# Own pools for the first two weight tiles behind each norm, converted ahead of the norm on VectorE

## The chip, the core and the metric

The kernel runs on one core of a Trainium2 chip. Five engines work there side by side, each on an instruction stream of its own: TensorE (PE) multiplies matrices, VectorE (DVE), ScalarE (ACT) and GpSimd (POOL) work element by element, and SyncE (SP) issues most of the transfers. Engines wait for each other by semaphores, and each takes its own instructions strictly in order. The metric is the device time of one execution in microseconds (us); lower is better.

## The reference

One inference step of a small recurrent decoder: 528 prompt positions (16 meta tokens and 512 new ones) and 8 running sequences of 8 tokens, so 592 positions with 1024 channels. Layer 0 has an S5 mixer, layer 1 a gated linear recurrence (RG-LRU). A post-norm and a gated feed-forward net with a causal width-3 convolution follow each mixer:

```python
mix = s5_mixer(h, ...)  or  rglru_mixer(h, ...)
h = layer_norm(DN_ALPHA * h + mix, g0, b0)
up = h @ w_up                                    # 1024 -> 2 * 2816
upc, new_hist = causal_dwconv(up, hist, conv_w, conv_b)
f = (gelu(upc[..., 2816:]) * upc[..., :2816]) @ w_down
h = layer_norm(DN_ALPHA * h + f, g1, b1)
```

All is float32, and the outputs are the hidden states and the new recurrent and convolution states.

## The kernel before

The kernel keeps activations transposed: a tile holds 128 channels by 592 positions, eight tiles (`RES`) hold the residual. Columns are worked in two halves of about 296. To get float32 accuracy from TensorE, each operand is cut into two parts, `hi` and `lo`; a product of two tiles is three matmuls (lines 151 to 153): `hi*hi`, `lo*hi` and `hi*lo`. Weights come as raw float32 tiles of 128 x 8 x 128 (`wraw`, a ring of three, loaded on SP's queue). Their `whi` is a copy on ScalarE (`convert_hi`, line 122), their `wlo` a subtraction (`convert_lo`, line 131), on VectorE unless the caller names GpSimd; both have rings of four. `keys` lists the weight tiles in the order of use; `load(to)`, `convert(to)` and `pump` work down that list to a given place, and `weights(key)` hands out the next.

There are four norms: behind the S5 mixer (I call it norm 0), behind the first feed-forward net (norm 1), behind the RG-LRU (norm 2), and the last. The first three are followed by another product. `skewed` (line 1005) writes the order by hand (`tc.manual_schedule`) so that one half of the columns is normed while TensorE works on the other half. Its steps:

- the first halves of the last `tail` tiles of the product (four, in norm 0 two) and their evacuation into `RES` (`evac`). `norm.add` squares each on ScalarE (L902) and adds up values and squares on GpSimd (L906, L907);
- the second halves on TensorE, and between them the totals over channels (`mean`, `square`: L920, L922);
- `centered` (line 924): mean and variance on ScalarE (L930, L931, L936) and VectorE (L934, L935, L951 to L955), the mean taken off `RES` (L940 on GpSimd, L945 on VectorE). `late` is called behind L936;
- `applied` (line 982): for each of eight tiles the scaling on VectorE (L973), `hi` on ScalarE (L974) and `lo` on VectorE (L979). `plan` says what stands behind tile k: the evacuations of the second halves, and conversions of weights;
- the first three output tiles of the next product (`nxt`, kept in `opened`): the first two take each `hi`, `lo` pair as it comes, with the totals of the second half behind the fifth pair, then the third; then `centered` and `applied` for the second half, and the second half of the three outputs.

Before the change, the weights of these three outputs are converted inside the norm: `whi` of the first two in `late`, and their `wlo` by `plan`, two on GpSimd in norm 0, one on GpSimd and one on VectorE in norms 1 and 2. The third is converted behind tile 5 or 6, its `wlo` on GpSimd. That makes seven conversions on GpSimd, 181 on VectorE.

Each feed-forward net opens a pool of its own (`ffn`, line 1125). Its first tile, `hist`, is loaded on ScalarE's queue (L1134) and prepared by four operations on GpSimd (L1138 to L1141); L1161 adds it to the convolution's result, and the gelu (L1166) follows. Behind each of the first three norms, GpSimd adds an offset to the eight tiles of `RES` (L1002). Outside `skewed` a scheduler sets each engine's order.

Of the kernel before, what the change touches and what calls it, by code (L numbers as in the profile page):

```python
# [9 lines left out]
F32R = mybir.dt.float32r  # L10
I32 = mybir.dt.int32
AF = mybir.ActivationFunctionType
ALU = mybir.AluOpType

P = 128
# [50 lines left out]
def trunk(tc, x, xn, s5p, s5bc, smp, fhist, w5i, w5o, wri, wrg, wro, wup, wdn, o_y, o_s5, o_rgh, o_rgc, o_ffc):  # L66
    nc = tc.nc
    V, G, A, T = nc.vector, nc.gpsimd, nc.scalar, nc.tensor
    with ExitStack() as ctx:
# [33 lines left out]
        keys = [("s5in", m) for m in range(DM)]  # L103
        for m in range(DM):
            keys += [("s5out", m), ("s5out", m + DM)]
        keys += ffn_keys(0) + rg_keys() + ffn_keys(1)
        raw, ready = {}, {}
        at = {"load": 0, "hi": 0, "conv": 0, "get": 0}

        def load(to):  # L110
            while at["load"] < min(to, len(keys)):
# [3 lines left out]
                raw[at["load"]] = (t, kk)  # L115
                at["load"] += 1

        def convert_hi(to):
            while at["hi"] < min(to, len(keys)):
                t, kk = raw[at["hi"]]  # L120
                hi = wp.tile([P, 8, P], F32R, tag="whi", name="whi", bufs=4)
                A.activation(hi[:, 0:kk, :], t[:, 0:kk, :], AF.Copy)  # L122
                ready[at["hi"]] = [hi, None]
                at["hi"] += 1

        def convert_lo(to, eng=V):
            while at["conv"] < min(to, len(keys)):
                t, kk = raw.pop(at["conv"])
                hi = ready[at["conv"]][0]
                lo = wp.tile([P, 8, P], F32R, tag="wlo", name="wlo", bufs=4)  # L130
                eng.tensor_tensor(lo[:, 0:kk, :], t[:, 0:kk, :], hi[:, 0:kk, :].bitcast(F32), op=ALU.subtract)  # L131
                ready[at["conv"]][1] = lo
                at["conv"] += 1
# [871 lines left out]
        def skewed(ms, prod, evac, norm, cols, hl, nxt, n, cuts, plan, slots=None, out=None, tail=4):  # L1005

            body, end = ms[:-tail], ms[-tail:]
            for m in body:
                if slots is not None:
                    whole(slots, m, cols)
                for f in (lambda h: prod(m, h, 0, n), lambda h: evac(m, h)):
                    for h in (0, 1):
                        f(h)

            def pair(i, h):
                if slots is not None and i < 2:  # L1020
                    ps = psum()
                    for j in (0, 1):
                        slots[end[i + 2 * j], h] = ps[:, 512 * j:512 * j + cols[h][1] - cols[h][0]]

            opened = []
            turn = list(order)
            with tc.manual_schedule():
                for i, m in enumerate(end):
                    pair(i, 0)
                    prod(m, 0, 0, n, ahead=i < tail // 2)  # L1030
                    evac(m, 0)
                load(at["conv"] + 3)
                A.activation(scr, scr, AF.Abs_reciprocal_sqrt)
                m = end[0]
                pair(0, 1)
                prod(m, 1, 0, cuts[0])
                norm.pst = psum()
                norm.mean(cols[0])
                prod(m, 1, cuts[0], cuts[1])
                norm.square(cols[0])  # L1040
                prod(m, 1, cuts[1], n)
                pair(1, 1)
                prod(end[1], 1, 0, n)
                early = (lambda: evac(m, 1)) if tail == 4 else None
                norm.centered(cols[0], late=plan.get("late"), early=early)
                if tail == 4:
                    prod(end[2], 1, 0, n)

                def second(i):
                    evac(end[i], 1)  # L1050
                    if tail == 4 and i == 1:
                        prod(end[3], 1, 0, n)

                todo = {k: [f if callable(f) else lambda i=f: second(i) for f in fs]
                        for k, fs in plan.items() if isinstance(k, int)}
                norm.applied(cols[0], hl, out, todo)
                c = cols[0]
                for i, key in zip((turn[1], turn[3]), nxt):
                    opened.append((psum(i), weights(key, False)))
                norm.pst = psum(turn[2])  # L1060
                for k in range(DM):
                    for o in opened:
                        part(*o, hl, c, k, k + 1, k == 0, k == DM - 1)
                    if k == 4:
                        norm.mean(cols[1])
                        norm.square(cols[1])
                if nxt:
                    opened.append((psum(turn[0]), weights(nxt[2], False)))
                    part(*opened[2], hl, c)
                order.remove(turn[2])  # L1070
                order.insert(0, turn[2])
                norm.centered(cols[1], lambda: A.activation(scr, scr, AF.Abs_reciprocal_sqrt))
                norm.applied(cols[1], hl, out)
                if nxt:
                    load(at["conv"] + 3)
                    convert(at["conv"] + 1)
                c = cols[1]
                for k in range(4):
                    for o in opened:
                        part(*o, hl, c, k, k + 1, k == 0, False)  # L1080
                for o in opened:
                    part(*o, hl, c, 4, DM, False, True)
            if hl is not None:
                norm.offsets(cols[0][0])
            return opened
# [10 lines left out]
        def convert(to, eng=V):  # L1096
            convert_hi(to)
            convert_lo(to, eng)
# [9 lines left out]
        def glu_evac(m, h):  # L1108
# [8 lines left out]
        HL1 = hltiles()  # L1117
        up_first = lambda l: [("up", l, m) for m in (0, FT, 1)]
        opened = skewed(list(range(DM)), glu_prod, glu_evac, norm, FULL, HL1, up_first(0), DM, (4, 4),
                        {"late": lambda: (A.activation(scr, scr, AF.Tanh), convert_hi(at["conv"] + 2)),  # L1120
                         0: [lambda: convert_lo(at["hi"], G)], 1: [0], 3: [1],
                         5: [lambda: convert(at["conv"] + 1, G)]}, tail=2)


        def ffn(l, *args):
# [3 lines left out]
        def ffn_in(fp, l, HL, u0, d0, i_norm, hl_out, opened, nxt, out):  # L1129
# [57 lines left out]
            for g, (k0, k1) in enumerate(GROUPS):  # L1187
# [44 lines left out]
                                PLAN if nxt else {0: [1], 3: [2], 4: [3]}, slots, out)  # L1232
            return hl, opened

        PLAN = {"late": lambda: convert_hi(at["conv"] + 2),
                0: [lambda: convert_lo(at["conv"] + 1, G), 1, lambda: convert_lo(at["conv"] + 1)],
                3: [2], 4: [3], 6: [lambda: convert(at["conv"] + 1, G)]}
        HL2, opened = ffn(0, HL1, 0, 0, 1, True, opened, [("rgin", DM + m) for m in range(3)], None)


# [151 lines left out]
        for m in range(3):  # L1392
            for h in (0, 1):
                ro_prod(m, h, DM - 2, DM)
            for h in (0, 1):
                ro_evac(m, h)
        HL3 = hltiles()
        opened = skewed(list(range(3, DM)), ro_prod, ro_evac, norm, gcols, HL3, up_first(1), DM, (4, 6), PLAN, slots)
        nc.sync.dma_start(o_rgc, rgc)
        nc.sync.dma_start(o_rgh, rgh)  # L1400
        rgs.close()

        pairs = {}

# [100 lines left out]
```

## Time and profile before

| what | before |
|---|---|
| median of 3 runs | 1402.8 us (1402.67 to 1412.2) |
| profiled execution | 1403.13 us, its span 1401.3 us |
| mean granted TensorE clock | 0.980 |
| PE busy | 1333.1 us (95%), 10680 instructions |
| DVE busy | 840.2 us (60%) |
| ACT busy | 582.7 us (42%) |
| POOL busy | 301.1 us (21%) |
| chain that ended last | PE 76%, DVE 17%, ACT 4%, issue 2%, POOL 1% |

The span is the time from the first to the last instruction. Busy times are sums over the span, so they don't tell which engine is late in a given stretch; for that the rows further down give single stretches, and the idle time ahead of an instruction with what ended it. The clock is a share of TensorE's 2.4 GHz; at 0.5 it runs at 1.2 GHz. Matmuls overlap in the records, so a busy TensorE is one that was not waiting.

### The profile page before, as it was taken

What the parts mean: (1) busy time and instruction counts of PE and PEld (TensorE: products, weight loads), DVE (VectorE), ACT (ScalarE), POOL (GpSimd) and SP (SyncE); (2) the same over time, 40 slices, a digit from 0 to 9 for tenths busy, and PEclk for the clock granted to TensorE, in tenths of its full rate; (3) what the DMA queues carried; (4) which work ended last, traced back from release to release, by engine and by line L of the source; (5) the groups of instructions that cost most, each with busy time, mean ns of one, the idle gap of its engine ahead of it and who ended that gap; (6) DMA issues with size and microseconds to landing.
All of it is one profiled execution on the core that took longest, in us unless ns stands there. A gap on an engine that the chain in (4) does not pass through costs nothing.

```text
span 1401.3 us, 25545 instructions
## 1 busy us (share of the span) xinstructions
PE 1333.1 (95%) x10680; PEld 1308.4 (93%) x10680; DVE 840.2 (60%) x1421; ACT 582.7 (42%) x942; POOL 301.1 (21%) x368
## 2 busy tenths in 40 slices
PE   6979889999999999999998999998999999999995
PEld 6978889988999999999998999998999999999994
DVE  8758936358655255535547889849655245535546
ACT  3645534235343133313433587734444124313433
POOL 1313402247000000000037431167100000000036
PEclk9979979999999999999999999999999999999998
DMA  6525554211322222222221212221322222222211
GB/s 221 162 82 138 132 177 136 76 61 61 106 76 84 83 76 85 67 91 91 66 82 61 93 45 92 96 68 61 107 90 77 90 78 85 74 97 81 77 52 68
DMA packets 72035, 127.65 MB, mean 91 GB/s; under 512 B 21232, under 2 KB 43888, under 8 KB 71920
## 3 DMA queue, kind: packets, MB, share of 16 engines
q1 hardware_dynamic: 62160, 120.45, 27.1%
q10 hardware_dynamic: 9760, 5.57, 1.4%
q8 instruction: 84, 1.38, 0.4%
q14 instruction: 31, 0.25, 0.1%
HBM read 113.35 MB, written 12.66 MB: 90 GB/s over the span
## 4 chain that ended last, share of the span: by engine, by line
PE 76%; DVE 17%; ACT 4%; issue 2%; POOL 1%; DMA 0%; SPq 0%; DVEq 0%; ACTq 0%
PE mm L152 24%; PE mm L153 24%; PE mm L151 24%; DVE wlo L131 2%; DVE res L973 1%; DVE lo L979 1%; PE mm L656 1%; DVE xw L542 1%; DVE res L945 1%; PE mm L660 1%; PE mm L605 1%; DVE t L635 1%; ACT res L479 1%; DVE res L968 1%; ACT whi L122 1%
## 5 line engine op out<-in xcount | busy, mean ns | idle before, releaser
L152 PE MATMUL mm<-lo,whi 128*128 128x296 f32 (+2 forms) x2816 | 843.9, 300 | 17.9 <-DVE lo L979 9.8
L151 PE MATMUL mm<-hi,whi 128*128 128x296 f32 (+2 forms) x2816 | 845.4, 300 | 13.8 <-ACT whi L122 6.8
L153 PE MATMUL mm<-hi,wlo 128*128 128x296 f32 (+2 forms) x2816 | 842.7, 299 | 2.8 <-DVE wlo L131 2.8
L152 PEld LDWEIGHTS mm<-lo,whi 128*128 128x128 f32 x2816 | 535.2, 190 | 23.9 <-DVE lo L979 14.5
L151 PEld LDWEIGHTS mm<-hi,whi 128*128 128x128 f32 x2816 | 535.1, 190 | 16.5 <-ACT whi L122 6.8
L153 PEld LDWEIGHTS mm<-hi,wlo 128*128 128x128 f32 x2816 | 534.7, 190 | 4.0 <-DVE wlo L131 4.0
L131 DVE TENSOR_TENSOR wlo<-wraw,whi 128x1024 fp32r<-128x1024 f32 (+1 forms) x181 | 228.2, 1265 | 220.0 <-ACT whi L122 219.3
L122 ACT ACTIVATE whi<-wraw 128x1024 fp32r<-128x1024 f32 (+1 forms) x188 | 194.5, 1039 | 302.5 <-PE mm L152 297.5
L1161 POOL TENSOR_TENSOR tmp<-tmp,hist 128x16 f32<-128x16 f32 x88 | 20.5, 235 | 697.4 <-DVE tmp L1158 697.4
L1156 DVE SCALAR_TENSOR_TENSOR tmp<-mm,sm,tmp 128x512 f32<-128x512 f32 (+2 forms) x176 | 132.1, 750 | 0.0
L1160 ACT ACTIVATE stg<-mm 128x18 f32<-128x18 f32 x88 | 16.4, 186 | 185.6 <-DVE tmp L1158 185.5
L1208 DVE TENSOR_TENSOR res<-mm,res 128x296 f32<-128x296 f32 (+3 forms) x48 | 26.0, 558 | 80.5 <-PE mm L153 80.5
L1151 ACT ACTIVATE tmp<-mm,sm 128x592 f32<-128x592 f32 (+1 forms) x88 | 72.2, 822 | 0.0
L1167 DVE TENSOR_TENSOR tmp<-tmp 128x592 f32<-128x592 f32 (+1 forms) x44 | 33.8, 767 | 38.7 <-ACT tmp L1166 38.7
L906 POOL TENSOR_TENSOR s<-s,res 128x296 f32<-128x296 f32 (+2 forms) x45 | 41.8, 930 | 60.9 <-DVE res L1114 31.2
L168 DVE TENSOR_TENSOR lo<-tmp,hi 128x592 fp32r<-128x592 f32 (+2 forms) x48 | 36.7, 764 | 29.6 <-ACT hi L167 29.6
L550 POOL TENSOR_TENSOR v<-cq,ap 128x512 f32<-128x512 f32 x32 | 42.5, 1359 | 49.8 <-ACT cq L494 41.1
L167 ACT ACTIVATE hi<-tmp 128x592 fp32r<-128x592 f32 (+2 forms) x48 | 33.1, 690 | 43.9 <-DVE tmp L1167 30.0
L1002 POOL TENSOR_SCALAR res<-res,sm 128x592 f32<-128x592 f32 (+1 forms) x24 | 49.2, 2065 | 6.3 <-DVE lo L979 6.3
L907 POOL TENSOR_TENSOR s<-s,tmp 128x296 f32<-128x296 f32 (+2 forms) x53 | 50.4, 955 | 0.2 <-ACT tmp L902 0.2
L902 ACT ACTIVATE tmp<-res 128x296 f32<-128x296 f32 (+2 forms) x56 | 24.0, 445 | 58.0 <-DVE res L1208 24.7
L1206 DVE SCALAR_TENSOR_TENSOR res<-res,mm 128x592 f32<-128x592 f32 (+1 forms) x16 | 12.2, 762 | 59.2 <-PE mm L153 59.2
(277 smaller groups left out, 1237.4 us busy)
## 6 DMA issues: line engine op xcount, KB each, us to landing
wraw<-in_wup SPq DMA_DIRECT2D x88, 512.0 KB, 3.4
wraw<-in_wdn SPq DMA_DIRECT2D x32, 448.0 KB, 3.3
wraw<-in_w5o SPq DMA_DIRECT2D x16, 512.0 KB, 4.3
wraw<-in_wdn SPq DMA_DIRECT2D x16, 512.0 KB, 3.5
wraw<-in_wri SPq DMA_DIRECT2D x16, 512.0 KB, 3.6
wraw<-in_w5i SPq DMA_DIRECT2D x8, 512.0 KB, 4.4
td<-lagsb SPq DMA_DIRECT2D x8, 512.0 KB, 3.4
lagged<-td SPq DMA_DIRECT2D x8, 512.0 KB, 4.2
```

Source lines behind the costliest of these rows:

```text
L122: A.activation(hi[:, 0:kk, :], t[:, 0:kk, :], AF.Copy)
L131: eng.tensor_tensor(lo[:, 0:kk, :], t[:, 0:kk, :], hi[:, 0:kk, :].bitcast(F32), op=ALU.subtract)
L151: T.matmul(out, hi[:, k, :], xh, start=start, stop=False)
L152: T.matmul(out, hi[:, k, :], xl, start=False, stop=False)
L153: T.matmul(out, lo[:, k, :], xh, start=False, stop=stop)
L168: V.tensor_tensor(lo[:, scols], src[:, scols], hi[:, scols].bitcast(F32), op=ALU.subtract)
L550: G.tensor_tensor(v[:, m], c[:, a, :, :, None].to_broadcast(sh), b[:, NQ * q:NQ * q + NQ, None, 1:CH + 1].to_broadcast(sh), op=ALU.mult)
L906: G.tensor_tensor(self.s1[:, cs_], RES[0][:, cs_] if m == 1 else self.s1[:, cs_], z, op=ALU.add)
L907: G.tensor_tensor(self.s2[:, cs_], self.s2[:, cs_], sq[:, cs_], op=ALU.add)
L1002: G.tensor_scalar(z, z, bm, None, op0=ALU.add)
L1151: A.activation(acc[:, d0:NT], X(d0, NT), AF.Identity, scale=w[2], bias=fcb[:, l, m:m + 1])
L1156: V.scalar_tensor_tensor(acc[:, a:TP], X(a - sh, TP - sh), w[k], acc[:, a:TP], op0=ALU.mult, op1=ALU.add)
```

## The change

Three things are changed. The first two weight tiles of `nxt` get `whi` and `wlo` in a pool of their own (`own0`, `own1`, `own2`, tags `xwhi` and `xwlo`), opened for the length of `skewed`. They are converted behind the evacuations of the last two first halves, `wlo` on VectorE. The third tile's `whi` is made in `late`, its `wlo` on VectorE behind the last `lo`. No conversion is left on GpSimd. `rgs.close()` moves ahead of the third `skewed`, so that the room of the RG-LRU's tiles can be taken. Lines behind the new function `room` have higher numbers in the changed kernel: L131 is L136 there, L1208 is L1220, L934 is L939.

```diff
+        def room(i, name):
+            if i in beside:
+                return beside[i].tile([P, 8, P], F32R, tag=f"x{name}", name=name, bufs=2)
+            return wp.tile([P, 8, P], F32R, tag=name, name=name, bufs=4)
+
         def convert_hi(to):
...
-                hi = wp.tile([P, 8, P], F32R, tag="whi", name="whi", bufs=4)
+                hi = room(at["hi"], "whi")
...
-                lo = wp.tile([P, 8, P], F32R, tag="wlo", name="wlo", bufs=4)
+                lo = room(at["conv"], "wlo")
...
-            with tc.manual_schedule():
+            with ExitStack() as ex:
+                if nxt:
+                    own = ex.enter_context(tc.tile_pool(name=f"own{norm.i}", bufs=1))
+                    beside.update({keys.index(key): own for key in nxt[:2]})
+                ex.enter_context(tc.manual_schedule())
                 for i, m in enumerate(end):
                     pair(i, 0)
                     prod(m, 0, 0, n, ahead=i < tail // 2)
                     evac(m, 0)
+                    if nxt and i >= tail - 2:
+                        load(at["conv"] + 3)
+                        convert(at["conv"] + 1)
                 load(at["conv"] + 3)
...
-                        {"late": lambda: (A.activation(scr, scr, AF.Tanh), convert_hi(at["conv"] + 2)),
-                         0: [lambda: convert_lo(at["hi"], G)], 1: [0], 3: [1],
-                         5: [lambda: convert(at["conv"] + 1, G)]}, tail=2)
+                        {"late": lambda: (A.activation(scr, scr, AF.Tanh), convert_hi(at["conv"] + 1)),
+                         1: [0], 3: [1], 8: [lambda: convert_lo(at["hi"])]}, tail=2)
...
-        PLAN = {"late": lambda: convert_hi(at["conv"] + 2),
-                0: [lambda: convert_lo(at["conv"] + 1, G), 1, lambda: convert_lo(at["conv"] + 1)],
-                3: [2], 4: [3], 6: [lambda: convert(at["conv"] + 1, G)]}
+        PLAN = {"late": lambda: convert_hi(at["conv"] + 1), 0: [1], 3: [2], 4: [3],
+                8: [lambda: convert_lo(at["hi"])]}
...
+        rgs.close()
         HL3 = hltiles()
         opened = skewed(list(range(3, DM)), ro_prod, ro_evac, norm, gcols, HL3, up_first(1), DM, (4, 6), PLAN, slots)
         nc.sync.dma_start(o_rgc, rgc)
         nc.sync.dma_start(o_rgh, rgh)
-        rgs.close()
```

TensorE's order stays as it was; the other engines' orders change at the norms and shortly behind. The first place is VectorE ahead of norm 1: evacuations of the residual's tiles 3 to 7 (`res_70` to `res_74`), then the norm's first own instruction. Before:

```order
L1208 TENSOR_TENSOR res_70<-mm,res_70 128x296 x2
L1208 TENSOR_TENSOR res_71<-mm,res_71 128x296
L131 TENSOR_TENSOR wlo<-wraw,whi 128x896
L1208 TENSOR_TENSOR res_72<-mm,res_72 128x296
L1208 TENSOR_TENSOR res_73<-mm,res_73 128x296
L1208 TENSOR_TENSOR res_74<-mm,res_74 128x296
L934 TENSOR_TENSOR tmp<-mm,tmp 128x296
```

And with the change:

```order
L1220 TENSOR_TENSOR res_71<-mm,res_71 128x296
L136 TENSOR_TENSOR wlo<-wraw,whi 128x896
L1220 TENSOR_TENSOR res_72<-mm,res_72 128x296
L1220 TENSOR_TENSOR res_73<-mm,res_73 128x296
L136 TENSOR_TENSOR wlo<-wraw,whi 128x1024
L1220 TENSOR_TENSOR res_74<-mm,res_74 128x296
L136 TENSOR_TENSOR wlo<-wraw,whi 128x1024
L939 TENSOR_TENSOR tmp<-mm,tmp 128x296
```

One conversion now stands between the last two evacuations and one behind the last, ahead of L934 (now L939); on ScalarE a `whi` stands behind the square of each.

The second place is GpSimd in norm 0, from the end of the first half's centering to the start of the second half's (`s_2579` and `s_2580` are the sums). Before:

```order
L940 TENSOR_TENSOR res_74<-res_74,tmp 128x296
L131 TENSOR_TENSOR wlo<-wraw,whi 128x1024 x2
L906 TENSOR_TENSOR s_2579<-s_2579,res_73 128x296
L907 TENSOR_TENSOR s_2580<-s_2580,tmp 128x296
L906 TENSOR_TENSOR s_2579<-s_2579,res_74 128x296
L907 TENSOR_TENSOR s_2580<-s_2580,tmp 128x296
L131 TENSOR_TENSOR wlo<-wraw,whi 128x1024
L940 TENSOR_TENSOR res_71<-res_71,tmp 128x296
```

And with the change:

```order
L945 TENSOR_TENSOR res_74<-res_74,tmp 128x296
L911 TENSOR_TENSOR s_2579<-s_2579,res_73 128x296
L912 TENSOR_TENSOR s_2580<-s_2580,tmp 128x296
L911 TENSOR_TENSOR s_2579<-s_2579,res_74 128x296
L912 TENSOR_TENSOR s_2580<-s_2580,tmp 128x296
L945 TENSOR_TENSOR res_71<-res_71,tmp 128x296
```

The three conversions are gone, and GpSimd goes from the centering straight to the sums.

The third place is VectorE in norm 1, between the last `lo` of the first half and the second half's norm. Before:

```order
L973 SCALAR_TENSOR_TENSOR res_74<-res_74,sm,tmp 128x296
L979 SCALAR_TENSOR_TENSOR lo<-res_73,sm,hi 128x296
L979 SCALAR_TENSOR_TENSOR lo<-res_74,sm,hi 128x296
L934 TENSOR_TENSOR tmp<-mm,tmp 128x296
L935 TENSOR_SCALAR tmp<-tmp 128x296
```

And with the change:

```order
L984 SCALAR_TENSOR_TENSOR lo<-res_73,sm,hi 128x296
L984 SCALAR_TENSOR_TENSOR lo<-res_74,sm,hi 128x296
L136 TENSOR_TENSOR wlo<-wraw,whi 128x1024
L939 TENSOR_TENSOR tmp<-mm,tmp 128x296
L940 TENSOR_SCALAR tmp<-tmp 128x296
```

The third output's `wlo` came from GpSimd to this place. Two more moves follow from the pools: the feed-forward pool of nets 0 and 1 lies where the own pool was, so the load of `hist` on ScalarE's queue now stands behind the norm, with a wait for TensorE, and GpSimd's four operations on it stand behind the eight L1002, ahead of the first L1161.

## Rows read from the trace of the kernel before

**Rows 1.** Table of stages: stretch, length, busy us (instructions) by engine, TensorE's clock, DMA.

```profile
295.00:345.00 50.00, 44.30 (x283) 41.38 (x283) 44.27 (x71) 27.53 (x46) 36.00 (x25) 0.93 0.16 53
...
345.00:395.00 50.00, 50.00 (x369) 50.00 (x368) 31.06 (x49) 21.85 (x34) 3.85 (x11) 1.00 0.29 95
...
738.00:788.00 50.00, 44.18 (x296) 41.09 (x295) 42.18 (x70) 24.68 (x43) 41.03 (x34) 1.00 0.16 55
...
938.00:988.00 50.00, 45.91 (x309) 43.75 (x309) 42.92 (x73) 26.63 (x47) 37.11 (x29) 0.97 0.18 57
```

**Rows 2.** Timeline of TensorE, norm 0: start, us, engine, line, operation [idle before].

```profile
328.26 0.41 PE L151 MATMUL mm<-hi,whi 128*128 128x296 f32 x1 [0.86 <-ACT hi L974]
```

**Rows 3.** Timeline of VectorE in norm 0 (x2: two instructions in one row).

```profile
303.66 2.66 DVE L955 SCALAR_TENSOR_TENSOR tmp<-tmp 128x296 f32<-128x296 f32 x1
...
306.36 2.98 DVE L973 SCALAR_TENSOR_TENSOR res<-res,sm,tmp 128x296 f32<-128x296 f32 x2
...
319.93 2.73 DVE L979 SCALAR_TENSOR_TENSOR lo<-res,sm,hi 128x296 fp32r<-128x296 f32 x2 [0.24 <-ACT hi L974]
...
326.62 0.45 DVE L955 SCALAR_TENSOR_TENSOR tmp<-tmp 128x296 f32<-128x296 f32 x1
...
327.11 0.97 DVE L973 SCALAR_TENSOR_TENSOR res<-res,sm,tmp 128x296 f32<-128x296 f32 x2
```

**Rows 4.** Timeline of GpSimd: its conversions in norm 0 and norm 1.

```profile
303.60 4.97 POOL L131 TENSOR_TENSOR wlo<-wraw,whi 128x1024 fp32r<-128x1024 f32 x2 [0.56 <-ACT whi L122]
...
762.96 2.38 POOL L131 TENSOR_TENSOR wlo<-wraw,whi 128x1024 fp32r<-128x1024 f32 x1 [2.80 <-ACT whi L122]
```

**Rows 5.** Timeline of ScalarE in norm 0.

```profile
298.77 0.42 ACT L930 ACTIVATE tmp<-mm 128x296 f32<-128x296 f32 x1 [0.80 <-PE mm L920]
```

**Rows 6.** Timeline of VectorE in norm 1.

```profile
740.29 0.47 DVE L1208 TENSOR_TENSOR res<-mm,res 128x296 f32<-128x296 f32 x1 [2.38 <-PE mm L153]
...
750.89 3.03 DVE L131 TENSOR_TENSOR wlo<-wraw,whi 128x1024 fp32r<-128x1024 f32 x1
...
763.35 2.31 DVE L979 SCALAR_TENSOR_TENSOR lo<-res,sm,hi 128x296 fp32r<-128x296 f32 x1 [0.68 <-ACT hi L974]
...
765.58 0.45 DVE L934 TENSOR_TENSOR tmp<-mm,tmp 128x296 f32<-128x296 f32 x1
```

**Rows 7.** Timeline of VectorE in norm 2.

```profile
938.03 0.45 DVE L1384 SCALAR_TENSOR_TENSOR res<-res,mm 128x282 f32<-128x282 f32 x1 [2.69 <-PE mm L153]
...
948.41 3.05 DVE L131 TENSOR_TENSOR wlo<-wraw,whi 128x1024 fp32r<-128x1024 f32 x1
...
960.70 2.32 DVE L979 SCALAR_TENSOR_TENSOR lo<-res,sm,hi 128x282 fp32r<-128x282 f32 x1 [0.70 <-ACT hi L974]
...
962.95 0.45 DVE L934 TENSOR_TENSOR tmp<-mm,tmp 128x296 f32<-128x296 f32 x1
```

**Rows 8.** Timeline of ScalarE in norm 1 (two rows) and norm 2.

```profile
737.95 0.45 ACT L902 ACTIVATE tmp<-res 128x296 f32<-128x296 f32 x1 [1.78 <-DVE res L1208]
...
764.02 0.42 ACT L930 ACTIVATE tmp<-mm 128x296 f32<-128x296 f32 x1 [0.70 <-PE mm L922]
...
961.38 0.42 ACT L930 ACTIVATE tmp<-mm 128x296 f32<-128x296 f32 x1 [0.71 <-PE mm L922]
```

**Rows 9.** View of tile whi: line, engine, count, ns min/median/max, first and last start.

```profile
L122 ACT ACTIVATE whi<-wraw x188: 935/1058/1073, 5.7 to 1362.8; 128x1024 fp32r<-128x1024 f32 x156, 128x896 fp32r<-128x896 f32 x32
L131 DVE TENSOR_TENSOR wlo<-wraw,whi x181: 1085/1226/3047, 10.2 to 1363.8; 128x1024 fp32r<-128x1024 f32 x149, 128x896 fp32r<-128x896 f32 x32
```

**Rows 10.** Views of lines L1134 (landing) and L1138 (as rows 9).

```profile
DMA to landing us min/median/max: 3.6/3.7/3.7
...
L1138 POOL TENSOR_TENSOR hist<-hist,sm x2: 853/853/853, 216.6 to 911.0; 128x352 f32<-128x352 f32 x2
```

**Rows 11.** Timelines of GpSimd and ScalarE behind norm 0.

```profile
328.87 17.86 POOL L1002 TENSOR_SCALAR res<-res,sm 128x592 f32<-128x592 f32 x8 [2.87 <-DVE lo L979]
...
347.13 0.70 ACT L1166 ACTIVATE tmp<-tmp 128x592 f32<-128x592 f32 x1 [3.35 <-POOL tmp L1161]
```

More of the change, by code (lines that the diff above doesn't have):

```diff
@@ L106, in trunk @@
         keys += ffn_keys(0) + rg_keys() + ffn_keys(1)
-        raw, ready = {}, {}
+        raw, ready, beside = {}, {}, {}
         at = {"load": 0, "hi": 0, "conv": 0, "get": 0}
```

## The prediction

> **What bounds the kernel now.** I read the table of stages first, then the timelines of TensorE, VectorE (DVE), ScalarE (ACT) and GpSimd (POOL) around each norm. In a stage like 345 to 395 us TensorE is busy all 50.00 of 50 us, 369 products, so 0.1355 us from one to the next. In the three 50 us windows that hold a norm with products behind it, it is busy 44.30, 44.18 and 45.91 us [rows 1]. These windows are all that the change can reach: 5.70 + 5.82 + 4.09 = 15.6 us of idle time. The granted clock there is 0.93, 1.00 and 0.97: some 7 us at the 1.2 GHz level in the first, 3 us in the third, which costs at most half of that, 5 us; in both, TensorE had been idle in pieces just before, in the same window.
>
> Who is late in these windows? The first product of a norm's second half waits for `hi` (L974), which waits for DVE [rows 2]. DVE works almost without a pause there, and some of its instructions are far longer than their like. In norm 0 L955 took 2.66 us, against 0.45 in the second half; the first two L973 took 2.98 together against 0.97; two L979 took 2.73 [rows 3]. In norm 1 the conversion (L131) took 3.03 and the last L979 2.31; in norm 2 3.05 and 2.32 [rows 6, 7]. All of them lie beside a POOL conversion: 303.60 to 308.57, and 762.96 to 765.34 [rows 4]. The L979 that started at 763.35 ended at 765.66, 0.32 us behind POOL.
>
> **What the change does, part by part.** I call the three norms N0 (295 us), N1 (738) and N2 (938), and use the lines of before.
>
> *Seven POOL conversions go* (three in N0, two each in N1 and N2). POOL's own time there is nobody's bound; what counts is what they do to DVE. N0: 2.66 - 0.45 = 2.21 at L955, 2.98 - 0.97 = 2.01 at the L973 pair, 2.73 - 0.97 = 1.76 at the L979 pair: 5.98 us. N1: 2.31 - 0.49 = 1.82 at the last L979, N2: 2.32 - 0.49 = 1.83 (0.97 / 2 = 0.49, for L979 reads and writes tiles of the same shape as L973). The other rows in which DVE is stretched, by POOL's L940 and its sums, stay.
>
> The Trainium skill (SBUF — State Buffer, section "SBUF: two separate sides") says of the port pair that the two engines share that whichever starts first holds it for its whole instruction and the other is fully blocked, a DVE instruction with two SBUF inputs included. By that rule the whole of the 1.82 goes; if they only shared bandwidth, an L979 would at most double and 0.49 would go. The 2.31 that ended 0.32 behind POOL agrees with the rule. The rule also speaks against the change: the conversions that now stand on DVE ahead of the norm can block POOL's sums.
>
> *One DVE conversion leaves the path of N1 and N2* (L131 between L1208 and the second L973): 3.03 and 3.05 us, since two of the three conversions are now made ahead of the norm.
>
> *One ScalarE conversion leaves the second half's way*: the `whi` that stood ahead of the last `hi`. DVE waited 0.24, 0.68 and 0.70 us for that `hi` [rows 3, 6, 7].
>
> *One DVE conversion is new on the path*: the third output's `wlo`, POOL's before, now stands behind the last L979 and ahead of L934. Median of 181: 1.226 us [rows 9]. Its bounds are 1.09 and 3.05; I take 1.23, since POOL waits for the norm's second mean there and has nothing to run before ScalarE gives it that.
>
> *Two conversions ahead of each norm.* Each costs 1.06 on ScalarE and 1.23 on DVE [rows 9], behind the evacuations of the last two tiles. Queued behind them are: on DVE the evacuation of the last tile (its sum on POOL and the mean on TensorE wait for that), on ScalarE the table load and L930. N0: the second `whi` fills the 0.80 us that ScalarE had idle before L930 [rows 5]; 1.06 - 0.80 = 0.26 late. N1: square 0.45 [rows 8], `whi` 1.06 and `wlo` 1.23 make 2.74 against the 2.38 us that DVE had idle ahead of the last evacuation [rows 6]: 0.36 late. There POOL is working through a backlog of sums, so one of its additions can come between: bounds 0.36 and 0.36 + 1.23 = 1.6; I take 1.0. N2: 2.74 against 2.69 [rows 7], 0.05, with a POOL addition perhaps 0.3; I take 0.3. The bound for all: 1.06 + 3.05 = 4.1 each.
>
> *More room.* The two outputs have their own pools, so the rings of four serve the others; the number of loads and conversions is the same and their order on the DMA queue too. Nothing here was waiting on the ring, so I cost it at nothing.
>
> *The histories come later.* The feed-forward pool now lies where the own room was. So the load of `hist` stands on ScalarE's queue behind the last read of the own weights, and POOL's four operations on it (0.853 us for the first [rows 10]; 3.4 us in all) stand behind the eight L1002, not before the norm. In before the gelu of the first pair started at 347.13 after waiting 3.35 us for POOL, whose L1002 ran from 328.87 for 17.86 us [rows 11]. Now: L1002 ends 4.7 earlier, at 342.0; plus 3.4 is 345.4; the gelu starts near 345.8. The DMA isn't late: it took 3.7 us to land [rows 10], and can be issued once TensorE has read the own weights, 60 products into the second half, at 328.26 - 4.73 + 60 x 0.1355 = 331.7. Behind the gelu on ScalarE is the release of the third PSUM tile. TensorE needs that after 72 + 3 x 48 = 216 products, 29.3 us from the start of the second half at 328.26 [rows 2], so at 357.5 in before and 352.8 now. Hidden, with 6 us to spare; if that cover were gone, each us would cost one.
>
> **The sum.** N0: 5.98 + 0.24 - 1.23 - 0.26 = 4.73 us. N1 by DVE: 3.03 + 0.68 + 1.82 - 1.23 - 1.0 = 3.30, so L934 at 762.28 instead of 765.58. But L934 also needs L930, which waits for TensorE: 764.02 moves by 3.03 - 1.0 = 2.03 to 761.99, and ends 0.42 later, at 762.41 [rows 8]. The gain is 765.58 - 762.41 = 3.17: what is late next is the total on TensorE. N2 the same way: DVE would give 3.05 + 0.70 + 1.83 - 1.23 - 0.3 = 4.05; L930 moves from 961.38 by 2.75 to 958.63, ends 959.05, and 962.95 - 959.05 = 3.90. Together 11.80 us. Behind each norm TensorE is the bound again, so a later start there is a later end.
>
> The profiled execution of before took 1403.13 us (its span 1401.3); 1403.13 - 11.8 = 1391.3. The median of the runs shown is 0.3 lower, so I forecast 1391.0 us.
>
> **The rivals.** *A: the head start is lost ahead of the norm.* The two conversions and POOL's sums block each other, and the last evacuation comes late. For it: N1's sums are back to back when the conversion comes, and the skill's lock works both ways. Against it: in N0 and N2 DVE had 2.7 us and more idle there. Price: 4.1 us in each norm instead of 0.26, 1.0 and 0.3, so 12.3 - 1.6 = 10.7 of the 11.8 go; with all of it 1402, with half 1396.5.
>
> *B: all the idle time goes.* The head start in the first half keeps TensorE fed and its clock at the upper level. That gives 15.6 us, and up to 20.6 with the clock: 1387 to 1382. For it: the stalls of the first half are those of DVE. Against it: the third `wlo` and the table load stay between the halves, so about 1 us of waiting should remain in each norm.
>
> *C: slower.* The gelu behind the late histories blocks ScalarE, whose in-order queue holds the PSUM release. It decides once POOL's operations on `hist` end over 6 us later than I place them; to eat the gain of 11.8 too, both feed-forward stages must lose another 5.9 each. At 15 us late the loss is 2 x 9 = 18 us, so 1409. Against it: the load's own time to land, 3.7 us.
>
> *D: no change*, since DVE is so busy that the conversions taken off POOL fill it again: seven of 1.23 are 8.6 us. For N0 to N2 three of them are counted on the path; were the other four there as well, 4.9 us go: 1396. Against it: DVE waits 2.4 to 2.7 us for TensorE between those evacuations.
>
> **Chances and range.** Forecast (gain 8 to 14): 0.55. A and D together (gain 1 to 8): 0.24. B: 0.16. C: 0.05. The likeliest case's own range is 1389 to 1395. The range 1387 to 1400 takes in the milder part of B and nearly all of A and D, and leaves out under 0.2. I take 1% (14 us) as about what a measurement of this kernel can tell from no change. Faster by over 1% means below 1388.8: B and the upper edge of the forecast, 0.22. Slower by over 1% needs C at its worst: 0.02. Within 1%: 0.76.
>
> **What would show it.** Right: no DVE row of L955, L973 or L979 above 1.2 us in the norms; N0's L973 pair near 0.97; TensorE's idle time in the three windows near 2 us each; no conversion on POOL; L934's second start 3 to 5 us earlier after the norm's begin. Wrong: the last evacuation ahead of the mean over 1.5 us late with TensorE waiting at L920 (A); a wait of TensorE within 30 us behind a norm on PSUM or `whi` (C); the granted clock at the lower level in a norm where it wasn't.

## The result, and the profile after

The changed kernel takes 1390.5 us (median; 1386.0 to 1391.2), before 1402.8: a ratio of 0.9889, interval 0.9843 to 0.9935. A second set of runs beside before on one chip gave 1391.5 against 1403.1, ratio 0.9915 (0.9898 to 0.9932). Forecast: 1391.0.

All lines from here on are those of the changed kernel: L131 of before is L136, L902/L906/L907 are L907/L911/L912, L920/L922 L925/L927, L930/L931/L934 L935/L936/L939, L940/L945 L945/L950, L955 L960, L973/L974/L979 L978/L979/L984, L1002 L1007, L1161/L1166 L1173/L1178, L1208 L1220; TensorE's products are L156 to L158.

The table of stages of the changed kernel (columns as in [rows 1]), for the three norms and the stretch behind N0:

```profile
290.00:340.00 50.00, 46.51 (x313) 44.23 (x313) 42.16 (x74) 26.57 (x45) 32.68 (x24) 0.97 0.21 72
730.00:780.00 50.00, 46.37 (x319) 43.85 (x318) 45.67 (x80) 26.35 (x46) 36.12 (x31) 1.00 0.19 64
925.00:975.00 50.00, 48.15 (x341) 46.30 (x341) 40.59 (x73) 23.79 (x42) 36.73 (x30) 1.00 0.24 82
340.00:390.00 50.00, 50.00 (x370) 50.00 (x369) 31.02 (x50) 21.95 (x36) 4.59 (x14) 1.00 0.26 86
```

TensorE fits 313, 319 and 341 products into 50 us, where [rows 1] had 283, 296 and 309: 30, 23 and 32 more, at 0.1355 us each 4.1, 3.1 and 4.3 us. The same comes out product by product. TensorE runs its 10680 products in one order in before and after, so the start of the same product can be subtracted: over N0 the changed kernel gains 4.0 us, over N1 2.9, over N2 4.2, in all 11.1. Outside the norms this one execution (1386.0 us, the fastest of the four) is ahead by another 6.2: 5.0 before the first norm, 1.2 between 785 and 915 us. The run *again*, below, shows that these are not the change's. The medians of the two sets are 12.3 and 11.6 us apart.

VectorE's timeline in the changed kernel, first half of N0, then the end of the first half in N0, N1 and N2:

```profile
298.70 0.45 DVE L960 SCALAR_TENSOR_TENSOR tmp<-tmp 128x296 f32<-128x296 f32 x1
299.19 0.96 DVE L978 SCALAR_TENSOR_TENSOR res<-res,sm,tmp 128x296 f32<-128x296 f32 x2
...
311.60 1.22 DVE L136 TENSOR_TENSOR wlo<-wraw,whi 128x1024 fp32r<-128x1024 f32 x1
313.50 0.47 DVE L939 TENSOR_TENSOR tmp<-mm,tmp 128x296 f32<-128x296 f32 x1 [0.69 <-ACT tmp L936]
...
751.62 0.53 DVE L984 SCALAR_TENSOR_TENSOR lo<-res,sm,hi 128x296 fp32r<-128x296 f32 x1 [0.17 <-ACT hi L979]
752.07 1.22 DVE L136 TENSOR_TENSOR wlo<-wraw,whi 128x1024 fp32r<-128x1024 f32 x1
753.55 0.47 DVE L939 TENSOR_TENSOR tmp<-mm,tmp 128x296 f32<-128x296 f32 x1 [0.27 <-ACT tmp L936]
...
944.46 1.22 DVE L136 TENSOR_TENSOR wlo<-wraw,whi 128x1024 fp32r<-128x1024 f32 x1
945.99 0.47 DVE L939 TENSOR_TENSOR tmp<-mm,tmp 128x296 f32<-128x296 f32 x1 [0.31 <-ACT tmp L936]
```

L960 is back from 2.66 to 0.45 and the L978 pair from 2.98 to 0.96 [rows 3]; the last L984 takes 0.53 where it took 2.31 [rows 6]. The third conversion stands where the prediction put it, at 1.22 us, and VectorE then still waits a little for ScalarE.

ScalarE's timeline (N0, N1, the first gelu), then TensorE's (the mean of N1, the start of the second half in N0, N1, N2):

```profile
312.75 0.42 ACT L935 ACTIVATE tmp<-mm 128x296 f32<-128x296 f32 x1 [1.63 <-PE mm L925]
...
752.79 0.42 ACT L935 ACTIVATE tmp<-mm 128x296 f32<-128x296 f32 x1 [1.20 <-PE mm L927]
...
342.81 0.70 ACT L1178 ACTIVATE tmp<-tmp 128x592 f32<-128x592 f32 x1 [6.93 <-POOL tmp L1173]
```

```profile
733.51 0.77 PE L925 MATMUL mm<-s,ones 128*128 128x296 f32 x2 [0.62 <-POOL s L911]
...
319.28 0.40 PE L156 MATMUL mm<-hi,whi 128*128 128x296 f32 x1 [0.71 <-ACT hi L979]
...
759.41 0.41 PE L156 MATMUL mm<-hi,whi 128*128 128x296 f32 x1 [1.00 <-ACT hi L979]
...
951.77 0.40 PE L156 MATMUL mm<-hi,whi 128*128 128x296 f32 x1 [1.15 <-ACT hi L979]
```

What is late next is TensorE's total (L925, L927) in front of L935, and in N1 GpSimd's sum in front of the mean.

### The profile page after: what moved, and what is told of

It reads as the page before. It is cut to its first block, busy times and chain, and to the rows that moved or that the text cites. A ratio compares the mean times of both kernels' runs of the same rounds, so it can differ in the third digit from the quotient of the medians.

```text
span 1383.9 us, 25538 instructions
## 1 busy us (share of the span) xinstructions
PE 1324.0 (96%) x10680; PEld 1301.5 (94%) x10680; DVE 836.0 (60%) x1428; ACT 581.6 (42%) x942; POOL 285.2 (21%) x361
## 4 chain that ended last, share of the span: by engine, by line
PE 76%; DVE 17%; ACT 3%; issue 2%; POOL 1%; DMA 1%; SPq 0%; DVEq 0%; ACTq 0%
PE mm L158 24%; PE mm L157 24%; PE mm L156 24%; DVE res L978 1%; DVE wlo L136 1%; DVE lo L984 1%; PE mm L661 1%; DVE xw L547 1%; DVE res L950 1%; PE mm L610 1%; DVE tmp L1350 1%; DVE ini L1347 1%; DMA res<-in_x 1%; DVE t L640 1%; PE mm L665 1%
## 5 line engine op out<-in xcount | busy, mean ns | idle before, releaser
L156 PE MATMUL mm<-hi,whi 128*128 128x296 f32 (+2 forms) x2816 | 842.9, 299 | 11.4 <-ACT whi L127 6.8
L157 PE MATMUL mm<-lo,whi 128*128 128x296 f32 (+2 forms) x2816 | 840.8, 299 | 12.3 <-DVE lo L694 5.1
L158 PE MATMUL mm<-hi,wlo 128*128 128x296 f32 (+2 forms) x2816 | 840.5, 299 | 2.4 <-DVE wlo L136 2.4
L156 PEld LDWEIGHTS mm<-hi,whi 128*128 128x128 f32 x2816 | 532.8, 189 | 13.7 <-ACT whi L127 6.8
L158 PEld LDWEIGHTS mm<-hi,wlo 128*128 128x128 f32 x2816 | 532.5, 189 | 3.4 <-DVE wlo L136 3.4
L136 DVE TENSOR_TENSOR wlo<-wraw,whi 128x1024 fp32r<-128x1024 f32 (+1 forms) x188 | 233.9, 1249 | 219.7 <-ACT whi L127 219.0
L1173 POOL TENSOR_TENSOR tmp<-tmp,hist 128x16 f32<-128x16 f32 x88 | 19.5, 224 | 686.6 <-DVE tmp L1170 686.5
L1220 DVE TENSOR_TENSOR res<-mm,res 128x296 f32<-128x296 f32 (+3 forms) x48 | 25.9, 557 | 78.1 <-PE mm L158 78.1
L1007 POOL TENSOR_SCALAR res<-res,sm 128x592 f32<-128x592 f32 (+1 forms) x24 | 54.5, 2287 | 6.2 <-DVE lo L984 6.2
L911 POOL TENSOR_TENSOR s<-s,res 128x296 f32<-128x296 f32 (+2 forms) x45 | 40.2, 894 | 62.8 <-DVE res L1127 32.6
L912 POOL TENSOR_TENSOR s<-s,tmp 128x296 f32<-128x296 f32 (+2 forms) x53 | 51.6, 978 | 0.0
L907 ACT ACTIVATE tmp<-res 128x296 f32<-128x296 f32 (+2 forms) x56 | 24.0, 445 | 56.6 <-DVE res L1220 24.3
```

The source lines that it names most:

```text
L156: T.matmul(out, hi[:, k, :], xh, start=start, stop=False)
L157: T.matmul(out, hi[:, k, :], xl, start=False, stop=False)
L158: T.matmul(out, lo[:, k, :], xh, start=False, stop=stop)
L911: G.tensor_tensor(self.s1[:, cs_], RES[0][:, cs_] if m == 1 else self.s1[:, cs_], z, op=ALU.add)
L912: G.tensor_tensor(self.s2[:, cs_], self.s2[:, cs_], sq[:, cs_], op=ALU.add)
L1007: G.tensor_scalar(z, z, bm, None, op0=ALU.add)
```

## The experiments

Two theories. **Block**: a GpSimd conversion stops VectorE, so what counts is that none is left on GpSimd. **Place**: what counts is that conversions stand ahead of the norm. The table gives the time and, by the subtraction above, what each kernel gains on before's trace in each norm (us; minus is a loss):

| run | median | N0 | N1 | N2 | sum |
|---|---|---|---|---|---|
| changed kernel, first trace | 1390.5 | 4.0 | 2.9 | 4.2 | 11.1 |
| the same, second trace (again) | 1391.5 | 4.8 | 2.8 | 4.1 | 11.8 |
| all on VectorE, old places | 1401.6 | 0.8 | -0.1 | 0.4 | 1.1 |
| ahead, but on GpSimd | 1394.4 | 4.5 | -0.1 | 3.4 | 7.8 |
| plus idle subtractions | 1407.7 | -0.6 | -2.6 | -0.3 | -3.6 |
| plus idle one-input work | 1392.9 (one) | 4.5 | 2.5 | 3.8 | 10.8 |
| plus idle memsets | 1399.7 (one) | 4.9 | 2.9 | 4.2 | 11.9 |
| third on GpSimd | 1404.7 | 1.8 | -0.8 | 2.1 | 3.1 |
| histories early | 1393.0 | 4.0 | 2.9 | 4.2 | 11.0 |
| one tile earlier | 1392.1 | 4.9 | 1.9 | 3.7 | 10.4 |
| totals earlier | 1390.6 | 4.9 | 3.4 | 4.7 | 12.9 |

Of before, 23 runs beside all on VectorE, ahead but on GpSimd, idle subtractions and third on GpSimd had a median of 1403.0, 9 beside again, histories early, one tile earlier and totals earlier 1403.1, and one beside the two kernels with a single run 1402.9. A time and a sum can differ by what the stage ahead of N0 does in an execution: at 290 us the traces of the memsets and of the third on GpSimd are 7.8 us behind before, that of again 9.4.

**The changed kernel again.**

> The changed kernel itself, once more. In the first traces it is 17.3 us ahead of the kernel before, 5.0 of them in the stage ahead of the first norm, whose code is the same in both, and 1.2 between 785 and 915 us. The three norms make 11.1. Theory 'norms': the 5.0 us are the clock's in that one execution (in before TensorE was at half clock for 13.65 us around 90 to 104 us, in after not), so this trace should come out anywhere from level with before to 5 us ahead of it at 290 us, and 11 us ahead over the norms: a time of 1386 to 1392. Rival 'stage': the change speeds up the first stage too; then it is again 5 us ahead at 290 us, and 1386 is its usual time.

The traced execution took 1400.9 us, the longest of its five. Up to 290 us it is 14.4 us *behind* the changed kernel's first trace and 9.4 behind before, further than either theory put it; 'stage' falls. Stages of before, of the changed kernel, and of it again (the last number but two is TensorE's granted clock):

```profile
60.00:130.00 70.00, 60.87 (x780) 56.22 (x779) 47.68 (x86) 34.52 (x73) 16.12 (x18) 0.88 0.37 106
130.00:200.00 70.00, 61.18 (x1000) 55.72 (x996) 53.36 (x66) 32.06 (x62) 23.11 (x24) 0.94 0.56 148
```

```profile
60.00:130.00 70.00, 60.74 (x895) 55.66 (x893) 53.99 (x91) 38.42 (x81) 20.68 (x24) 0.98 0.44 126
130.00:200.00 70.00, 61.15 (x901) 56.10 (x900) 47.82 (x61) 28.80 (x56) 18.45 (x19) 0.86 0.56 159
200.00:290.00 90.00, 89.37 (x644) 89.06 (x644) 36.74 (x89) 31.19 (x49) 19.10 (x23) 0.98 0.31 100
```

```profile
60.00:130.00 70.00, 60.91 (x771) 56.20 (x771) 47.54 (x86) 34.39 (x82) 16.10 (x18) 0.88 0.38 108
130.00:200.00 70.00, 62.89 (x953) 57.60 (x951) 50.45 (x65) 29.30 (x56) 21.92 (x24) 0.83 0.48 127
200.00:290.00 90.00, 87.65 (x634) 86.69 (x634) 36.13 (x87) 32.15 (x50) 15.87 (x19) 0.92 0.39 124
```

One kernel had 0.98, 0.86 and 0.98 in one execution and 0.88, 0.83 and 0.92 in the next, so differences there belong to no edit. By these shares the second execution lacks 0.10 x 70 + 0.03 x 70 + 0.06 x 90 = 14.5 us of full clock, about what it is behind. Between 785 and 915 us it, and every other kernel here, is level with before within 0.1 us; the first trace's 1.2 us was that execution's. In the norms it gains 11.8. In N0 the clock was 1.00 instead of 0.97, and the four totals of the second half took 1.16 us where the first trace has 2.17 (first trace, then second):

```profile
310.53 2.17 PE L925 MATMUL mm<-s,ones 128*128 128x296 f32 x4
```

```profile
324.45 1.16 PE L925 MATMUL mm<-s,ones 128*128 128x296 f32 x4
```

**All on VectorE, at the old places.**

```
-  0: [lambda: convert_lo(at["hi"], G)], 1: [0], 3: [1], 5: [lambda: convert(at["conv"] + 1, G)]
+  0: [lambda: convert_lo(at["hi"])], 1: [0], 3: [1], 5: [lambda: convert(at["conv"] + 1)]
   (and so in PLAN, for N1 and N2)
```

> The kernel before, with its seven GpSimd conversions put on VectorE at the places where they stood; no own room, nothing ahead of the norm. Theory 'block': a GpSimd conversion stops VectorE for most of its length, so taking it off GpSimd pays although VectorE now does the work itself. N0: the stalls of 5.98 us (rows L955, first two L973, two L979 of [rows 3]) go and three conversions of 1.23 come: 5.98 - 3.69 = 2.3 us gained. N1 and N2: the last L979 falls from 2.31 to about 0.5 (1.82 gained), the L131 of 3.03 becomes two of 1.23 (0.57 gained), a third of 1.23 comes on the path: 1.2 us each. In all 4.7 us gained, 1398. Rival 'place': what pays is only that the conversions stand ahead of the norm; VectorE wasn't stopped by GpSimd. Then VectorE gets 3.7 us of work in N0 and 2.5 in each of the others on top of what it had: 6 to 8 us slower, 1410.

VectorE in N0 (lines of before):

```profile
304.80 0.45 DVE L955 SCALAR_TENSOR_TENSOR tmp<-tmp 128x296 f32<-128x296 f32 x1
305.29 0.53 DVE L973 SCALAR_TENSOR_TENSOR res<-res,sm,tmp 128x296 f32<-128x296 f32 x1
305.73 2.35 DVE L131 TENSOR_TENSOR wlo<-wraw,whi 128x1024 fp32r<-128x1024 f32 x2
...
318.69 1.23 DVE L131 TENSOR_TENSOR wlo<-wraw,whi 128x1024 fp32r<-128x1024 f32 x1 [1.12 <-ACT whi L122]
```

Every stretched row is gone, as 'block' has it, yet only 1.1 of the 4.7 us came; by the medians (1401.6 against 1403.0) that can't be told from nothing. VectorE now does the work, and ahead of the third conversion it waits 1.12 us for `whi` in each norm, a wait that GpSimd had borne. 4.7 less three times 1.12 is 1.3. Taking the conversions off GpSimd isn't enough: VectorE's work has to leave the norm too.

**Ahead of the norm, but on GpSimd.**

```
-  convert(at["conv"] + 1)          (behind the last two tiles)
+  convert(at["conv"] + 1, G)
```

> The changed kernel with the two conversions ahead of each norm on GpSimd; the third stays on VectorE. It asks whether 'ahead' is enough or 'not on GpSimd' matters there too. Theory 'block': each takes 2.4 to 5 us on GpSimd as in [rows 4] and stands ahead of the last sums of the first half, which the first mean on TensorE waits for; VectorE's evacuations beside it are stopped too. N1 and N2: two of 2.4, less the 0.6 us by which N1 is already late and the slack of the others, 3 to 4 us late each; N0 2 to 4. In all 8 to 12 us slower than the changed kernel, 1399 to 1402, the norms' later rows as in the changed kernel. Rival 'place': the conversions ahead are hidden on whichever engine, and the time is that of the changed kernel, 1390, within 2 us.

Neither: 3.3 us of 11.1 lost, most of it in N1. GpSimd and TensorE there:

```profile
734.58 2.36 POOL L136 TENSOR_TENSOR wlo<-wraw,whi 128x1024 fp32r<-128x1024 f32 x1
736.90 0.80 POOL L911 TENSOR_TENSOR s<-s,res 128x296 f32<-128x296 f32 x1
737.66 0.80 POOL L912 TENSOR_TENSOR s<-s,tmp 128x296 f32<-128x296 f32 x1
738.43 2.35 POOL L136 TENSOR_TENSOR wlo<-wraw,whi 128x1024 fp32r<-128x1024 f32 x1
...
737.75 1.27 PE L925 MATMUL mm<-s,ones 128*128 128x296 f32 x2 [1.95 <-POOL s L911]
```

The first conversion stands in front of the last sums, and the mean waits 1.95 us. The changed kernel's mean waited 0.62, so that is 1.3 of the 3.0 us that N1 loses; the rest comes right behind, where the granted clock fell (0.69 from 736 to 741 us): the two pairs of totals took 1.27 and 1.15 us, 0.77 and 0.66 in the changed kernel. In N0 and N2 GpSimd had time, and there 'place' nearly holds: N0 loses 0.3 us against the second trace, whose clock it shares (against the first it gains 0.5), N2 0.8.

**Idle work on GpSimd: subtractions, one input, none.** At the places of GpSimd's old conversions, on the changed kernel (shortened):

```
+  def busy():
+      d = spare[0].tile([P, 8, P], mybir.dt.bfloat16, tag="dum", name="dum")   # spare: the own room
+      o = ones[:, None, :].to_broadcast([P, 8, P])               # [P, 4, P] in the second run
+      G.tensor_tensor(d, o, o, op=ALU.subtract)                  # first run
+      G.tensor_scalar(d[:, 0:4, :], o, 1.0, None, op0=ALU.add)   # second run, instead
+      G.memset(d, 0.0)                                           # third run, instead
+  N0: 0: [busy, busy], 5: [busy];   N1, N2: 0: [busy, 1], 6: [busy]
```

> The changed kernel plus GpSimd subtractions of two 128x1024 inputs whose result nobody reads (three in N0, two each in N1 and N2), at the places where GpSimd's conversions stood before. Nothing waits for them but GpSimd itself. Theory 'block': the stalls come back on VectorE, beside the extra GpSimd rows: in N0 near 6 us in the rows of L960, L978 and L984, in N1 and N2 1.8 each at the last L984 and another 1 to 2 at the start; the run loses most of what the change gained in the norms, 8 to 11 us against the changed kernel: 1398 to 1402. Rival 'place': no row of VectorE changes, since no data depends on the extra work; the time is that of the changed kernel, 1390, within 2 us.

> The changed kernel plus GpSimd work that nobody reads, at the same places as in the run with idle subtractions, but with one input of 128x512 (an addition of a constant) instead of two of 128x1024, some 2 us each by the 2.34 us of L1007's 592 elements. Theory 'two inputs': it is the pair of inputs on both engines that stops VectorE; beside eight L1007 (one input, 2.34 us each) VectorE's L978 rows in after go from 0.52 to 0.94 at most. Then no VectorE row of L960, L978, L984 is above 1.2 us and the three norms lose under 2 us against the changed kernel (14.7 with the subtractions). Rival 'any work': every GpSimd instruction on SBUF stops VectorE for its length; rows of 2 us come back and the norms lose 10 us or more.

> The same with a GpSimd memset of 128x1024 at those places, which reads nothing. Theory 'two inputs': no stretched row on VectorE, norms within 1 us of the changed kernel's. Rival 'any work': VectorE rows stretched by the memset's length, and some us lost.

GpSimd, then VectorE in N0, with subtractions (lines are 5 higher: L965 is L960):

```profile
302.74 4.19 POOL L121 TENSOR_TENSOR dum<-ones 128x1024 bf16<-128x1024 f32 x2
...
303.39 1.78 DVE L965 SCALAR_TENSOR_TENSOR tmp<-tmp 128x296 f32<-128x296 f32 x1
305.21 2.48 DVE L983 SCALAR_TENSOR_TENSOR res<-res,sm,tmp 128x296 f32<-128x296 f32 x2
...
316.23 2.15 DVE L989 SCALAR_TENSOR_TENSOR lo<-res,sm,hi 128x296 fp32r<-128x296 f32 x1
```

and with one input (the last row stands beside the third addition):

```profile
302.95 3.49 POOL L121 TENSOR_SCALAR dum<-ones 128x512 bf16<-128x512 f32 x2
...
303.60 0.49 DVE L965 SCALAR_TENSOR_TENSOR tmp<-tmp 128x296 f32<-128x296 f32 x1
304.13 0.97 DVE L983 SCALAR_TENSOR_TENSOR res<-res,sm,tmp 128x296 f32<-128x296 f32 x2
...
313.66 0.87 DVE L989 SCALAR_TENSOR_TENSOR lo<-res,sm,hi 128x296 fp32r<-128x296 f32 x1
```

Subtractions that nobody waits for cost the norms 14.7 us, more than the whole gain, with stalls like those of [rows 3] at the same lines: 'block' is shown, and 'place' alone, which forecast no change here, falls. I had put the loss at 8 to 11. The stretched rows make 10.3 of it (4.5 in N0, 2.9 in N1 and in N2); the rest is that TensorE, which waits 1.99 us for an L989, then brings the totals late, so that L944 (L939) waits 2.87 us in N1 and 1.91 in N2, 0.27 and 0.31 in the changed kernel. With one input L965 and L983 are untouched. One L989 in each norm takes 0.87 (0.85 in N2), 0.36 more than its like, not the 1.7 us of the addition; 0.3 us goes against the first trace, 1.0 against the second. With a memset nothing does. The additions hold up GpSimd's own sums nearly as long as the subtractions (3.49 us against 4.19), so that isn't what costs 14.7 us.

SBUF is the memory that these tiles lie in; TensorE's outputs (`mm`) lie in another, PSUM. The Trainium skill (SBUF — State Buffer, "SBUF: two separate sides") has the two engines lock each other out where VectorE has two SBUF inputs and the GpSimd operation reads SBUF. The subtractions agree. The one-input addition reads SBUF too, 1.7 us each time, and lengthened at most one row by 0.36: for that form the measurement decides.

**The third conversion on GpSimd.**

```
-  8: [lambda: convert_lo(at["hi"])]
+  8: [lambda: convert_lo(at["hi"], G)]
```

> The changed kernel with the third output's wlo (the one behind the last L984) on GpSimd, as before the change. The prediction counted it on VectorE's path at 1.23 us in each norm. By that term the second half's L939 comes 1.23 us earlier if GpSimd does it, 3.7 in all: 1386.7. By the trace of after, L939 waits 0.69, 0.27 and 0.31 us for ScalarE (L936) behind that conversion, so taking it off brings nothing, and a GpSimd conversion of 2.4 to 5 us there stops L939 and L940 until it ends: L939 then ends 0.7 to 2 us later than in the changed kernel, 2 to 5 us in all: 1392 to 1395. If the conversion on GpSimd neither helps nor stops anything: 1390, within 1 us.

The sign is that of the second reading, the size and place aren't: 8.0 us lost. GpSimd, VectorE, then TensorE in N0:

```profile
321.21 2.56 POOL L136 TENSOR_TENSOR wlo<-wraw,whi 128x1024 fp32r<-128x1024 f32 x1
...
321.49 2.60 DVE L984 SCALAR_TENSOR_TENSOR lo<-res,sm,hi 128x296 fp32r<-128x296 f32 x1
...
324.15 0.61 PE L157 MATMUL mm<-lo,whi 128*128 128x296 f32 x1 [2.45 <-DVE lo L984]
```

It is the last conversion in VectorE's order, but GpSimd has a queue of its own: it starts as soon as the sum in front of it is done and `whi` is there, six operations of VectorE earlier, and stops an L984 in the middle of the half, for which TensorE waits 2.45 us. That stall makes 2.1 us in each norm, 6.2 of the 8.0. Nothing is saved behind it, since L939 waits for ScalarE even without the conversion, 1.92, 3.08 and 1.45 us; in N1 that is 1.7 more than conversion and wait had taken. The 1.23 us that VectorE pays is the cheap way.

**The histories early.** A room for the first block's histories, opened ahead of the norm:

```
+  hp = early.enter_context(tc.tile_pool(name="hp", bufs=1))
+  hist0 = [hp.tile([P, 2 * FT, 8, 2], F32, name="hist"), hp.tile([P, 2 * FT, 8], F32, name="th")]
...                              (net 0 takes its hist and th from hist0)
```

> The changed kernel with the histories of the first feed-forward block in a room of their own, opened ahead of the norm, so that their load and GpSimd's four operations on them no longer wait for the own weights' room. The prediction cost their late start at nothing: the gelu of the first pair would start some 3 us earlier, before 341 instead of 342.8, and TensorE not at all: the time from the first norm's end to 700 us is that of the changed kernel within 0.3 us, 1390 in all. Rival: the late histories cost something (rival C of the prediction, in small); then TensorE gains up to 3 us there. GpSimd's operations that come ahead of the norm again can take some of VectorE's time there, up to 1 us.

The gelu starts at 344.09 in a trace that is 6.0 us behind at that point, so 4.7 us earlier than in the changed kernel, where I expected some 3. TensorE gains nothing, as expected: from N0's end to 700 us it is level with the changed kernel within 0.03 us.

**The two conversions one tile earlier.**

```
-  if nxt and i >= tail - 2:
+  if nxt and tail - 2 <= i + (tail == 4) < tail:
```

> The changed kernel with the two conversions ahead of N1 and N2 behind the tiles one earlier each, so none behind the last tile's evacuation. In after TensorE waits 0.62 us in N1 for GpSimd's sum ahead of the mean (L911 under L925), which the conversions made late (rival A in small). Theory: that wait goes, since VectorE has 2.4 us idle ahead of each of these evacuations: N1 gains 0.6 to 0.7, N0 and N2 nothing, 1389.8. Rival: the conversions stop GpSimd's backlog of sums wherever they stand, and the wait stays, 1390.5.

Worse: N1 loses 1.0 us more, N2 0.5. GpSimd and TensorE in N1:

```profile
732.53 1.81 POOL L911 TENSOR_TENSOR s<-s,res 128x296 f32<-128x296 f32 x1
...
735.87 1.79 POOL L912 TENSOR_TENSOR s<-s,tmp 128x296 f32<-128x296 f32 x1
...
738.48 0.77 PE L925 MATMUL mm<-s,ones 128*128 128x296 f32 x2 [1.57 <-POOL s L911]
```

The block works both ways. A conversion on VectorE makes one sum on GpSimd 1.8 us instead of 0.82. In the changed kernel only one of the two falls into N1's backlog of sums:

```profile
730.87 1.82 POOL L912 TENSOR_TENSOR s<-s,tmp 128x296 f32<-128x296 f32 x1
```

Here both do, and the wait of 0.62 grows by 0.95.

**The totals one k earlier.**

```
-  if k == 4:
+  if k == 3:
       norm.mean(cols[1])
       norm.square(cols[1])
```

> The changed kernel with the totals of the second half (L925, L927 in the loop over k) one k earlier, k == 3. In after ScalarE's L935 waits 1.63 and 1.20 us for these totals on TensorE in N0 and N1, while GpSimd's last sum is 1.5 to 2 us older; then VectorE waits 0.69, 0.27 and 0.31 us for ScalarE at L939 behind the third conversion. Theory 'totals': TensorE sets the start of the second half; the first hi comes earlier by what VectorE had idle, 0.69, 0.27 and 0.31 us, and with VectorE then the bound no more: 1.3 us in all, 1389.2. Rival: the six products put behind the totals end later by as much as the second half starts earlier, or L935 isn't what VectorE waits for: no change, 1390.5.

N1 and N2 gain 0.5 each on the changed kernel; N0, against the second trace with the same clock, nothing. VectorE in N1:

```profile
756.11 1.22 DVE L136 TENSOR_TENSOR wlo<-wraw,whi 128x1024 fp32r<-128x1024 f32 x1
757.24 0.46 DVE L939 TENSOR_TENSOR tmp<-mm,tmp 128x296 f32<-128x296 f32 x1
```

L939 follows the conversion without a wait, 1.13 us after its start instead of 1.48. So the totals did set the second half in N1 and N2; in N0 only while the clock was low. By the sums this version beats both, by 1.1 us over the changed kernel; its median (1390.6 against 1391.5) is too close to tell.

## Why the prediction was right

- **The block** and its 5.98 us in N0, 1.82 and 1.83 in N1 and N2: shown. The rows fell to what their second-half like had, and the idle subtractions brought the stalls back. That the wait for the last `hi` (0.24, 0.68, 0.70) would go whole was wrong: 0.17 us of it are left in each norm.
- **The head start**: VectorE's first L939 came 0.04, 0.73 and 0.01 us late, where I had 0.26, 1.0 and 0.3.
- **N0**, 4.73 forecast: 4.0 in the first trace, 4.8 at the full clock. The missing 0.7 is the 0.69 us that L939 waited behind totals at half clock.
- **N1**, 3.17 forecast, 2.9 and 2.8 measured. The late mean, taken at 1.0 between 0.36 and 1.6, was a wait of 0.62, and of the kind named: one sum stretched on GpSimd. What that saved went elsewhere: I let L934 start when L930 ends, but it waits for L931 behind it, 0.34 us more (L939 starts at 753.55, L935 ends at 753.21). That the total in front of L930, not VectorE, is late next was right for N1, as the totals one k earlier show.
- **N2**, 3.90 forecast, 4.2 and 4.1 measured, but L939's second start came only 3.8 earlier: the 0.3 for a late mean was too much, since TensorE didn't wait there, and L936 was left out here too. The rest, in no term, arises behind it: TensorE ran 3.4 us of before's second half at half clock, its products 0.25 us apart (0.97 for the window in [rows 1]); the changed kernel's window is at 1.00.
- **The third conversion**, counted at 1.23 on VectorE's path: it took 1.22, partly under the wait for the totals.
- **The late histories**, cost at nothing: shown. The gelu came 23.5 us behind the second half's first product (342.81 - 319.28) where I had 22.3 (345.8 - 323.5), since eight L1007 took 18.95 us, not 17.86; within the 6 us of cover.
- **A reading that failed**: "these windows are all that the change can reach", 15.6 us of idle time, and its sign, idle time near 2 us in each. It is 3.5, 3.6 and 1.9, and fell by 6.6 us for a gain of 11.1. The busy column hides part of a wait: a product behind a stall is drawn at 0.40 us where in a row one starts every 0.1355, and products at half clock count as busy. So a busy TensorE isn't quite one that was not waiting, as I had it ahead of the prediction. The count of products gives the gain within 0.4 us; by it before lacked 86, 73 and 60 of the 369 that fit, 29.7 us, less what the longer totals need. Rival B's ceiling was too low for this reason.
- **The rivals**: A came in small, in N1 alone; B, C and D didn't. That the forecast of 1391.0 is within 0.5 us of the median owes some luck to the stage ahead of N0, and N2's part to the clock.

## What to carry to other kernels

Work that two engines can do isn't free on the idle one: look for rows of the busy engine that are several times their like, and for what the other engine ran beside them. Taking such work off the idle engine pays only if it also leaves the stretch in which the busy one sets the pace: here 1.1 us of 11 without that. Count a stage's products, not its idle time, and subtract the same product's start in two traces to see where a gain arises.

## What the runs showed of the hardware

- GpSimd's operations with two SBUF inputs stop VectorE's with two SBUF inputs until they end (L965 1.78, L989 2.15 beside the idle subtractions of 2.1 each); a one-input addition of 1.7 us lengthens one by at most 0.36, a memset of 0.95 none.
- Two VectorE operations with one of their two inputs in PSUM weren't stopped: in the changed kernel L950 (`res<-res,mm`) takes 0.45 us beside GpSimd's L945 (two SBUF inputs, 18 times) as with GpSimd idle, and L1220 (`res<-mm,res`) 0.45 to 0.47 beside the sums and without them.
- It holds in the other direction: a VectorE conversion of 1.2 us makes a sum on GpSimd 1.8 us instead of 0.8.
- The granted clock of the first 290 us differs from one execution to the next of the same kernel (0.98, 0.86, 0.98 and 0.88, 0.83, 0.92 in three stretches), which moved everything behind it by 14.4 us, more than the change.
